# Down projections with their two plain products first in each round, and the third tile of tokens finished one tile of sums sooner

## The chip, the cores and the metric

The kernel runs on one core of one Trainium2 chip. A core has five engines with a queue each: TensorE (PE) multiplies matrices, VectorE (DVE), ScalarE (ACT) and GpSimd (POOL) work on tiles, and SyncE (SP) issues most transfers between the device's memory and the on-chip buffer. Each queue is worked off in order, and engines wait for each other by semaphores. Sums of matrix products land in eight banks of 128 x 512 fp32, from which DVE and ACT read them. The metric is the device time of one execution in microseconds (us); of several runs the median is given.

## The reference

A decoder of two layers on 1024 tokens plus 16 meta tokens, all in fp32, width 1024. Layer 0 is a state-space mixer, layer 1 an attention; each is followed by a gated feed-forward part, and the result is normalized once more:

```python
def _conv_ffn(u, w_up, conv_w, conv_b, w_down):
    h = _causal_dwconv(u @ w_up, conv_w, conv_b)
    g, val = jnp.split(h, 2, axis=-1)
    return (jax.nn.silu(g) * val) @ w_down
...
        h = h + _conv_ffn(_rmsnorm(h, ffn_norm[layer]), ffn_w_up[layer], ffn_conv_w[layer],
                          ffn_conv_b[layer], ffn_w_down[layer])
    return _rmsnorm(h, final_norm)[:, N_META:]
```

The hidden width of the feed-forward part is 2816, that is 22 blocks of 128 rows. The change concerns the last product, `... @ w_down` (the down projection, run once for each layer), and the last line (the final norm) of the second layer.

## The kernel before, in words

**Precision.** Every fp32 matrix is split into a high and a low part (`wh`, `wl` for weights, `gh`, `gl` for tokens). A product of fp32 matrices is then three matmuls: high by high, high by low, low by high (`mm3`, lines 171 to 173). The high part is a copy on ACT; the low part is a subtraction of two tiles, on DVE for tokens (`gl`, L1057) and on POOL for weights (`wl`, L1055).

**A down projection** (`down`) works in two parts. The first 16 of the 22 blocks of rows are cut in two halves, and so are the tokens and the 1024 output columns; the product of these 2 x 2 blocks is made with seven block products instead of eight (Winograd's form of Strassen's scheme), numbered 1 to 7. The remaining six blocks of rows are multiplied plainly afterwards ("tiles of sums": four tiles of tokens, each with eight output blocks, `accumulate`, L403).

**The seven products.** Their operands are (tokens, weights): product 1 is (b11, a11) and product 2 is (b21, a12), the blocks as they were loaded. The others take sums and differences, which DVE makes in place, one after the other in a chain that starts with product 7: `a21 = a11 - a21` (L1039) and `b12 = b22 - b12` (L1040) for 7; `a21 = a22 - a21` (L1042) and `b11 = b11 + b12` (L1043) for 6; L1045 and L1046 for 5; L1048 for 3; L1050 for 4. The order before is 1, 7, 6, 5, 3, 4, 2.

**Rounds and sets.** The 16 blocks of rows are done in two rounds of two sets each (`Set`). In each round every product is done for set 0 and then for set 1; I call one product of one set a half product. `make` prepares the operands of one half product (the differences, `wh` and `wl`, `gh` and `gl`) while PE works on the half product before. There are three buffers each for `wh` and `wl`, so that the operands of a half product can be made only when the one three steps back is through PE. PE sums both sets of a product in the same bank, and at the second set the bank is taken over into the accumulator `acc` of that product: by a copy on ACT (L1102) where it is the first for 1, 5, 6 and 7, by an addition on DVE otherwise (L1104). The accumulators of products 2, 3 and 4 lie in `h`, which holds the residual stream and is loaded ahead of the second product (L1146).

**Banks.** In the first layer a half product has 8 groups of sums (two tiles of 260 tokens by four output blocks, 48 matmuls of 260 columns), which takes all eight banks. In the second layer it has 4 groups (24 matmuls of 512 columns), which takes four, and the products alternate between two lots of four banks.

**Loading.** `FIRST` is the order in which a set's eight blocks are loaded (g for tokens, w for weights); `NEXT` says behind which product which blocks of the next round are loaded, namely when their buffers have come free. All these transfers are in SP's queue, in order (L1025, L1030).

**After the products** the accumulators are added up (`sums`, L1074), and the four tiles of sums follow. After each tile `after` is called: in layer 1 it is `finish`, which for tiles 0, 1 and 2 calls `finish_tokens`: squares on ACT (L239), their sums on POOL and DVE, sums over the rows on PE (L1479), the factor 1/rms (`token_rstd`: L222, a logarithm and an exponential on ACT, L223 and L224, then L225 to L228), transposes on PE (L1487), scaling by the factor and by the gain (L1489, L1490, L1492), and a transfer to the output (L1493). Each tile of 256 tokens is two chunks of 128. The fourth tile is finished by `finish_last`, woven in with its own sums (L1508 to L1542).

**What sets the order.** The attention's order is written out by hand. Elsewhere a scheduler, which simulates the engines with its own durations, orders the instructions on each queue when the kernel is built. So the change also shows in the order of instructions on each queue, which I read from the built kernels.

Of the kernel before, what the change touches and what calls it, by code (L numbers as in the profile page):

```python
# [13 lines left out]
P = 128  # L14
# [37 lines left out]
FFN = Tokens(0, 0), Tokens(META, HB)  # L52
# [34 lines left out]
class Trunk:  # L87
# [905 lines left out]
    def down(self, layer, gd, hd, pool, after, each=None):  # L993
# [68 lines left out]
        def part(ps, op, f, t, first):  # L1062
            gh, gl, wh, wl = op
            for q in range(2):
                s0, n = wide[t]
                c, e = slice(q * H + f * P, q * H + f * P + P), slice(s0, s0 + n)
                self.mm3(ps[:, :n], wh[:, c], wl[:, c], gh[:, q, e], gl[:, q, e], first and q == 0, not first and q == 1)
# [6 lines left out]
                        behind(tt(acc[x, f], acc[x, f], acc[y, f], op=ADD), self.last_add, "behind the products")  # L1074
                        yield

        FIRST = ("g", 0, 0), ("w", 0, 0), ("g", 1, 1), ("g", 0, 1), ("w", 1, 0), ("w", 1, 1), ("w", 0, 1), ("g", 1, 0)

        NEXT = {5: FIRST[:2], 3: FIRST[2:3] + FIRST[4:5], 4: FIRST[3:4] + FIRST[5:6], 2: FIRST[6:]}
        rounds = [[Set(s) for s in (r, r + 1)] for r in range(0, NW // 2, 2)]  # L1080

        def load(sets, what):
            for kind, i, j in what:
                for x in sets:
                    (x.load_g if kind == "g" else x.load_w)(i, j)

        load(rounds[0], FIRST)
        h = [self.Q("h") for _ in range(KD)]
# [9 lines left out]
        def add(i, f, t, ps, first):  # L1098
            s0, n = wide[t]
            x = acc[i, f][:, s0 : s0 + n]  # L1100
            if first and i in (1, 5, 6, 7):
                nc.scalar.activation(x, ps[:, :n], AF.Copy)  # L1102
            else:
                self.last_add = tt(x, x, ps[:, :n], op=ADD)  # L1104
# [4 lines left out]
        def weights(b, hi, lo):  # L1109
            w32 = self.wp.tile([P, 1024], F32, tag="w32", name=self.nm("w32"))  # L1110
            nc.sync.dma_start(w32, a["w_down"][layer, b])
            nc.scalar.activation(hi, w32, AF.Copy)
            pt(lo, w32, hi.bitcast(F32), op=SUB)  # L1113
            ws.append((hi, lo))

        def tokens(x):

            us[x] = []
            for b in rows:
                t = self.Q("g", F32R)  # L1120
                hi, lo = t[:, :S], t[:, QW // 2 : QW // 2 + S]
                nc.sync.dma_start(lo.bitcast(F32), gd[b, :, S * x : S * x + S])
                nc.scalar.activation(hi, lo.bitcast(F32), AF.Copy)
                tt(lo, lo.bitcast(F32), hi.bitcast(F32), op=SUB)
                us[x].append((hi, lo))

        own = lambda: (pool.tile([P, 1024], F32R, tag=z, name=self.nm(z)) for z in ("fh", "fl"))
        common = lambda: (self.wp.tile([P, 1024], F32R, tag=z, name=self.nm(z)) for z in ("wh", "wl"))
        plan = [(r, i, x) for r in range(len(rounds)) for i in (1, 7, 6, 5, 3, 4, 2) for x in range(2)]
        made = {}  # L1130

        def make(n):
            if n < len(plan):
                r, i, x = plan[n]
                made[n] = rounds[r][x].operands(i)
                if r + 1 < len(rounds) and i in NEXT:
                    load([rounds[r + 1][x]], NEXT[i])

        make(0)
        for m in range(0, len(plan), 2):  # L1140
            r, i, _ = plan[m]
            last = r + 1 == len(rounds)
            ps = {}
            if r == 0 and i == 7:
                for f in range(KD):
                    nc.sync.dma_start(h[f][:, : 2 * S] if f < 4 else h[f][:, half(0)], hd[f] if f < 4 else hd[f, :, half(0)])  # L1146
            if last and i == 2:
                h22 = [self.Q("h22") for _ in range(2)]
                h22 = [h22[f // 2][:, f % 2 * S : f % 2 * S + S] for f in range(4)]
                for f in range(4):  # L1150
                    nc.sync.dma_start(h22[f], hd[4 + f, :, half(1)])
            for x in range(2):
                make(m + x + 1)
                if last and i == 4 and x:
                    weights(rows[0], *own())
                if last and i == 2 and not x:
                    tokens(0)
                    weights(rows[1], *own())
                    weights(rows[2], *(self.Q(z, F32R)[:, :D] for z in ("wh", "wl")))
                    for b in rows[3:]:  # L1160
                        weights(b, *common())
                for n, (t, f) in enumerate((t, f) for t in range(len(wide)) for f in range(4)):
                    if x == 0:
                        ps[t, f] = kinds[(m // 2 * 4 * len(wide) + n) % 8]("acc")
                    part(ps[t, f], made[m + x], f, t, x == 0)
                    if x == 1:
                        add(i, f, t, ps.pop((t, f)), r == 0)
                del made[m + x]
# [294 lines left out]
    def finish(self, h, j):  # L1463
        if j == 0:
            self.gfin = self.wp.tile([P, D], F32, tag="w32", name="gfin")
            self.nc.sync.dma_start(self.gfin, self.a["final_norm"].to_broadcast([P, D]))
        if j < 3:
            self.finish_tokens(h, [(t, P) for t in range(FFN[1].tile * j, FFN[1].tile * (j + 1), P)])

    def finish_tokens(self, h, chunks):  # L1470

# [160 lines left out]
```

## Time and profile before

| | us |
|---|---|
| median of 3 runs | 3002.04 |
| lowest and highest of them | 2996.2, 3002.11 |
| the profiled execution | 2999.73 |
| span of the profile | 2998.0 |
| first down projection, products | 1362 to 1538 |
| second down projection, products | 2732 to 2901 |
| its tiles of sums and the end | 2901 to 2998 |

The profile is one execution with start and duration of every instruction. A view by windows counts the instructions of a stretch and gives the TensorE clock that was granted (1.00 is full speed); the view of waits sums, for an instruction that stood idle, which instruction released it; the timeline lists instructions in order, with the idle time before them and its releaser in brackets; the chain of waits is the path that ended last. The profiled execution took 1.73 us more than its span, and 2.31 us less than the median.

### The profile page before, as it was taken

What the parts mean: (1) busy time and instruction counts of PE and PEld (TensorE: products, weight loads), DVE (VectorE), ACT (ScalarE), POOL (GpSimd) and SP (SyncE); (2) the same over time, 40 slices, a digit from 0 to 9 for tenths busy, and PEclk for the clock granted to TensorE, in tenths of its full rate; (3) what the DMA queues carried; (4) which work ended last, traced back from release to release, by engine and by line L of the source; (5) the groups of instructions that cost most, each with busy time, mean ns of one, the idle gap of its engine ahead of it and who ended that gap; (6) DMA issues with size and microseconds to landing.
All of it is one profiled execution on the core that took longest, in us unless ns stands there. A gap on an engine that the chain in (4) does not pass through costs nothing. (4 is left out here: it accounts for less than half of the span.)

```text
span 2998.0 us, 57316 instructions
## 1 busy us (share of the span) xinstructions
PE 2881.1 (96%) x21863; PEld 2737.4 (91%) x21863; DVE 2303.7 (77%) x4026; ACT 1646.3 (55%) x3403; POOL 1309.6 (44%) x1250
## 2 busy tenths in 40 slices
PE   7999999989998999999999999999899999998998
PEld 4999898979998999999999999999798999997878
DVE  5586868886369887878876888888739888888775
ACT  4555555553145556555334888888736555555433
POOL 1254444542334666663443222222343676673441
PEclk9999999999999999999999999999999999999999
DMA  5233333323222222235232122222332222225331
GB/s 162 69 107 90 105 95 100 108 69 135 70 75 70 79 75 82 79 99 180 64 126 84 55 65 62 65 69 55 123 122 65 78 80 84 78 75 173 105 104 59
DMA packets 123411, 272.72 MB, mean 91 GB/s; under 512 B 13664, under 2 KB 53216, under 8 KB 123136
## 3 DMA queue, kind: packets, MB, share of 16 engines
q1 hardware_dynamic: 117760, 257.93, 27.4%
q10 hardware_dynamic: 4112, 6.56, 0.7%
q8 instruction: 172, 2.82, 0.4%
q0 software_dynamic: 1264, 4.57, 0.4%
q14 instruction: 103, 0.84, 0.1%
HBM read 200.89 MB, written 53.20 MB: 85 GB/s over the span
## 5 line engine op out<-in xcount | busy, mean ns | idle before, releaser
L171 PE MATMUL pj<-uh,wh 128*128 128x348 f32 (+2 forms) x1536 | 505.5, 329 | 12.0 <-ACT bk L629 6.1
L172 PE MATMUL pj<-ul,wh 128*128 128x348 f32 (+2 forms) x1536 | 498.6, 325 | 0.0
L173 PE MATMUL pj<-uh,wl 128*128 128x348 f32 (+2 forms) x1536 | 495.9, 323 | 0.0
L171 PE MATMUL p<-bh,fh 128*128 128x262 f32 (+1 forms) x1408 | 401.4, 285 | 6.8 <-DVE c L296 2.8
L173 PE MATMUL p<-bh,fl 128*128 128x262 f32 (+1 forms) x1408 | 401.6, 286 | 3.4 <-POOL fl L905 3.4
L172 PE MATMUL p<-bl,fh 128*128 128x262 f32 (+1 forms) x1408 | 402.4, 286 | 0.1
L905 POOL TENSOR_TENSOR fl<-x,fh 128x1024 fp32r<-128x1024 f32 x88 | 212.5, 2416 | 259.8 <-ACT fh L904 207.6
L172 PE MATMUL p<-bl,wh 128*128 128x262 f32 (+1 forms) x1056 | 301.2, 285 | 6.2 <-DVE bl L857 6.1
L171 PEld LDWEIGHTS pj<-uh,wh 128*128 128x128 f32 x1536 | 292.1, 190 | 15.6 <-ACT xbc L293 4.6
L171 PE MATMUL p<-bh,wh 128*128 128x262 f32 (+1 forms) x1056 | 302.4, 287 | 0.9 <-ACT bh L856 0.9
L173 PE MATMUL p<-bh,wl 128*128 128x262 f32 (+1 forms) x1056 | 301.3, 285 | 0.0
L165 POOL TENSOR_TENSOR wl<-w,wh 128x1024 fp32r<-128x1024 f32 (+2 forms) x76 | 155.2, 2044 | 317.9 <-ACT wh L164 317.8
L172 PEld LDWEIGHTS pj<-ul,wh 128*128 128x128 f32 x1536 | 292.2, 190 | 1.7 <-issue 0.8
L173 PEld LDWEIGHTS pj<-uh,wl 128*128 128x128 f32 x1536 | 291.8, 190 | 1.0 <-issue 0.8
L296 DVE SCALAR_TENSOR_TENSOR c<-p,params,c 128x260 f32<-128x260 f32 (+1 forms) x528 | 250.4, 481 | 47.3 <-ACT c L293 36.9
L171 PEld LDWEIGHTS p<-bh,fh 128*128 128x128 f32 x1408 | 268.7, 191 | 7.9 <-ACT c L293 4.9
L173 PEld LDWEIGHTS p<-bh,fl 128*128 128x128 f32 x1408 | 268.7, 191 | 4.1 <-POOL fl L905 4.0
L172 PEld LDWEIGHTS p<-bl,fh 128*128 128x128 f32 x1408 | 268.1, 190 | 1.1 <-DVE bl L857 0.7
L947 DVE TENSOR_TENSOR c<-c,c 128x260 f32<-128x260 f32 (+1 forms) x176 | 242.0, 1377 | 5.0 <-ACT c L943 2.0
L952 ACT ACTIVATE ft<-p 128x262 f32<-128x262 f32 (+1 forms) x352 | 126.3, 382 | 204.3 <-DVE p L955 181.4
L1055 POOL TENSOR_TENSOR wl<-w,wh 128x1024 fp32r<-128x1024 f32 x56 | 147.5, 2637 | 207.9 <-ACT wh L1054 205.7
L172 PE MATMUL acc<-gl,wh 128*128 128x260 f32 (+1 forms) x672 | 217.9, 325 | 14.7 <-DVE gl L1057 14.7
(325 smaller groups left out, 8473.0 us busy)
## 6 DMA issues: line engine op xcount, KB each, us to landing
w<-in_w_up SPq DMA_DIRECT2D x88, 512.0 KB
w<-in_w_down SPq DMA_DIRECT2D x44, 512.0 KB
w<-in_w_in SPq DMA_DIRECT2D x40, 512.0 KB
E<-ea_d SPq DMA_DIRECT2D x32, 464.0 KB
D<-acs_d SPq DMA_DIRECT2D x32, 420.5 KB
g<-c SPq DMA_DIRECT2D x88, 130.0 KB
g<-c SPq DMA_DIRECT2D x88, 128.0 KB
b<-g SPq DMA_DIRECT2D x16, 520.0 KB
```

Source lines behind the costliest of these rows:

```text
L165: nc.gpsimd.tensor_tensor(wl[:, :n], w32[:, :n], wh[:, :n].bitcast(F32), op=ALU.subtract)
L171: mm(out, wh, uh, start=first, stop=False, skip_group_check=joins)
L172: mm(out, wh, ul, start=False, stop=False, skip_group_check=joins)
L173: mm(out, wl, uh, start=False, stop=last, skip_group_check=joins)
L296: nc.vector.scalar_tensor_tensor(out, ps[:, o + i : o + i + n], wcol(i), out, op0=ALU.mult, op1=ALU.add)
L905: tt(lo[:, :n], t, hi[:, :n].bitcast(F32), op=ALU.subtract)
L947: self.last_up = tt(g[:, :FN], g[:, :FN], v[:, :FN], op=ALU.mult)
L952: nc.scalar.activation(s[:, :N], ps[:, :N], AF.Copy)
L1055: pt(wl, y, wh.bitcast(F32), op=SUB)
```

## The change

It has two parts. The order of the products becomes 1, 2, 7, 6, 5, 3, 4; the loads follow: b21 and a12 come right after b11 and a11, and in the next round b21, a12 and a21 are loaded behind product 3, b22, b12 and a22 behind product 4. What was tied to the place of a product (loading `h` ahead of the second one, the last weights and tokens at the last one) keeps its place in the order. And `finish` is called with other tiles: after the second tile of sums it finishes tiles 0 and 1, after the third tile 2, after the fourth nothing. The computation is the same.

```diff
-        FIRST = ("g", 0, 0), ("w", 0, 0), ("g", 1, 1), ("g", 0, 1), ("w", 1, 0), ("w", 1, 1), ("w", 0, 1), ("g", 1, 0)
-
-        NEXT = {5: FIRST[:2], 3: FIRST[2:3] + FIRST[4:5], 4: FIRST[3:4] + FIRST[5:6], 2: FIRST[6:]}
+        PRODUCTS = 1, 2, 7, 6, 5, 3, 4
+        FIRST = ("g", 0, 0), ("w", 0, 0), ("g", 1, 0), ("w", 0, 1), ("g", 1, 1), ("g", 0, 1), ("w", 1, 0), ("w", 1, 1)
+
+        NEXT = {5: FIRST[:2], 3: FIRST[2:4] + FIRST[6:7], 4: FIRST[4:6] + FIRST[7:]}
...
-        plan = [(r, i, x) for r in range(len(rounds)) for i in (1, 7, 6, 5, 3, 4, 2) for x in range(2)]
+        plan = [(r, i, x) for r in range(len(rounds)) for i in PRODUCTS for x in range(2)]
...
-            if r == 0 and i == 7:
+            if r == 0 and i == 2:
...
-            if last and i == 2:
+            if last and i == 4:
...
-                if last and i == 4 and x:
+                if last and i == 3 and x:
...
-                if last and i == 2 and not x:
+                if last and i == 4 and not x:
...
-        if j < 3:
-            self.finish_tokens(h, [(t, P) for t in range(FFN[1].tile * j, FFN[1].tile * (j + 1), P)])
+        for i in {0: (0, 1), 1: (2,)}.get(j, ()):
+            self.finish_tokens(h, [(t, P) for t in range(FFN[1].tile * i, FFN[1].tile * (i + 1), P)])
```

Beside the three places that it touches, the two down projections and the end, the order of instructions on every queue is as before.

## The prediction

> **What bounds the kernel now.** The page's head says that TensorE is busy nearly all the time.
>
> ```profile
> span 2998.0 us, 57316 instructions
> PE 2881.1 (96%) x21863; PEld 2737.4 (91%) x21863; DVE 2303.7 (77%) x4026; ACT 1646.3 (55%) x3403; POOL 1309.6 (44%) x1250
> ```
>
> So only what lets PE stand, or slows it, can be won. I next read the view by windows for PE's matmuls into `acc`, cut at the down projections. Columns: the window, its length, busy time with the number of matmuls, then the granted clock.
>
> ```profile
> 1362.00:1408.00 46.00, 38.81 (x305) 0.96 0.36 124
> 1408.00:1460.00 52.00, 52.00 (x436) 1.00 0.43 134
> 1460.00:1500.00 40.00, 36.15 (x287) 0.96 0.04 14
> 2732.00:2793.00 61.00, 53.10 (x210) 0.92 0.40 135
> 2793.00:2870.00 77.00, 77.00 (x334) 1.00 0.19 62
> ```
>
> An undisturbed stretch of the first down projection does 436/52 = 8.38 matmuls per us, of the second 334/77 = 4.34. At these rates the 305 at its head need 36.4 us and took 46: **9.6 us lost**. The 210 need 48.4 and took 61: **12.6 us lost**. The 287 in round two need 34.2: 5.8 us lost. What PE waited for, first in the window 1300 to 1600, then in 2700 to 2998 (columns: total us, times, longest):
>
> ```profile
> PE acc L172 <- DVE gl L1057: 6.8, 3, 4.2
> PE acc L171 <- DVE p L1104: 3.9, 2, 2.2
> ```
>
> ```profile
> PE acc L172 <- DVE gl L1057: 7.9, 2, 4.9
> ```
>
> At the heads PE stands 6.8 and 7.9 us for the low part of a token operand; the rest of the losses (2.8 and 4.7) is the slow clock behind the waits, about 1 us a wait in the first and 2.3 in the second. In round two it stands 3.9 us for a bank that DVE has not yet added up. Both times DVE is late. Why it is late at the second head, from the timelines of DVE, POOL and ACT:
>
> ```profile
> 2733.68 2.75 DVE L947 TENSOR_TENSOR c<-c,c 128x256 f32<-128x256 f32 x2 [1.39 <-ACT c L943]
> 2737.72 1.22 DVE L1039 TENSOR_TENSOR w<-w,w 128x1024 f32<-128x1024 f32 x1
> 2738.86 1.22 DVE L1040 TENSOR_TENSOR b<-b,b 128x1024 f32<-128x1024 f32 x1
> ...
> 2741.13 3.44 DVE L1040 TENSOR_TENSOR b<-b,b 128x1024 f32<-128x1024 f32 x1
> 2744.49 3.36 DVE L1043 TENSOR_TENSOR b<-b,b 128x1024 f32<-128x1024 f32 x1
> 2747.77 1.21 DVE L1057 TENSOR_TENSOR gl<-b,gh 128x1024 fp32r<-128x1024 f32 x1
> ```
>
> ```profile
> 2733.42 2.40 POOL L1055 TENSOR_TENSOR wl<-w,wh 128x1024 fp32r<-128x1024 f32 x1 [18.10 <-ACT wh L1054]
> 2740.16 6.60 POOL L1055 TENSOR_TENSOR wl<-w,wh 128x1024 fp32r<-128x1024 f32 x2 [4.34 <-ACT wh L1054]
> 2806.82 2.40 POOL L1055 TENSOR_TENSOR wl<-w,wh 128x1024 fp32r<-128x1024 f32 x1 [2.81 <-ACT wh L1054]
> 2812.39 2.41 POOL L1055 TENSOR_TENSOR wl<-w,wh 128x1024 fp32r<-128x1024 f32 x1 [3.17 <-ACT wh L1054]
> ```
>
> ```profile
> 2732.28 1.06 ACT L1054 ACTIVATE wh<-w 128x1024 fp32r<-128x1024 f32 x1 [1.03 <-DMA w<-in_w_down]
> 2739.02 1.06 ACT L1054 ACTIVATE wh<-w 128x1024 fp32r<-128x1024 f32 x1 [4.92 <-issue]
> ```
>
> A DVE operation on two tiles follows the next at 1.14 us (2737.72 to 2738.86), but each of POOL's two `wl` makes one of them take 3.4: **they run by turns**, and each `wl` that falls among them costs DVE 2.25 us. So between 2737.72 and 2747.77 DVE did 5 operations (5.7) and paid for two `wl` (4.5). A half product is 2812.39 - 2806.82 = 5.57 us of PE here. In the first layer:
>
> ```profile
> 1367.48 1.22 DVE L1039 TENSOR_TENSOR w<-w,w 128x1024 f32<-128x1024 f32 x1
> 1429.76 2.09 DVE L1104 TENSOR_TENSOR h<-h,acc 128x260 f32<-128x260 f32 x6
> ...
> 1363.16 2.40 POOL L1055 TENSOR_TENSOR wl<-w,wh 128x1024 fp32r<-128x1024 f32 x1 [17.57 <-ACT wh L1054]
> 1430.29 2.40 POOL L1055 TENSOR_TENSOR wl<-w,wh 128x1024 fp32r<-128x1024 f32 x1 [3.38 <-ACT wh L1054]
> 1436.02 2.41 POOL L1055 TENSOR_TENSOR wl<-w,wh 128x1024 fp32r<-128x1024 f32 x1 [3.33 <-ACT wh L1054]
> ```
>
> A half product is 5.73 us (1436.02 - 1430.29), and six additions out of a bank take 0.35 each although a `wl` runs beside them: those do not take turns.
>
> **Part 1, second down projection.** No instruction is added or removed; product 2 moves ahead of 7. DVE gains two half products before PE asks for a difference, but in the built order of DVE's queue the low part for product 2, set 1 now stands eighth behind the end of the up projection: two L1039, two L1040, two L1043, one L1042, then it. (For set 0 it stands among the last operations of the up projection, with time to spare.) PE asks for it after three half products and eight matmuls that do without (as many stand ahead of it in PE's queue): 2732 + 3 x 5.57 + 8/4.34 = 2750.5. When is it there? POOL's second `wl` had to wait in the profile until ACT could begin at 2739.02, since product 1 held a buffer. Product 2's set 0 has a free buffer and weights that came early, so its `wl` now follows at once at 2735.8 and takes turns with the up projection's last L947, as 2733.68 shows (2.75 for two of 0.4). I let DVE start 2.1 us later, at 2739.8 (bounds: 0 and 4.5, one more `wl` in it). Eight operations: 2739.8 + 9.1 = 2748.9. Among them fall the `wl` of product 2 set 1 (from 2740.1), of product 7 set 0 (buffer free after two half products, 2743.1, plus ACT: 2744.3) and of 7 set 1 (2749.9): 3 x 2.25 = 6.8. So 2755.7, a wait of 5.2, with 2.3 for the clock: 7.5 of the 12.6 stay. Behind it, product 7's low parts are two and three operations later, in time, and product 6's after it, with 1 or 2 us to spare; its sums have banks of their own. **Gain 5.1**; bounds: 12.6 if DVE is in time (2739.8 less 2.1, one `wl` among the eight: 2749.0), 0 if two more `wl` come before it.
>
> **Part 1, first down projection.** The same, but the low part in question stands seventh, and PE asks for it at 1362.4 + 3 x 5.73 + 4/8.38 = 1380.1. DVE started at 1367.48; the moved `wl`, at 1365.6 behind the one at 1363.16, puts that off to about 1370.2. Then 7 x 1.14 = 8.0 and two `wl`: 1382.7, a wait of 2.6. PE is through with product 2 at 1388. Now the banks: product 7 needs the ones of product 2, all eight are in use, and they come free by DVE's L1105 (L1104 before) instead of ACT's copies, which did it for product 1. In DVE's built queue the first of these additions stands behind five more operations (two L1057, L1042, L1046, L1045): 1382.7 + 5.7 + 2.25 to 4.5 = 1390.7 to 1392.9. That is **a new wait** of 2.7 to 4.9, say 4. The other additions stand in two lots behind one to two operations, and PE has three groups of both sets to do meanwhile. With the clock, about 1 us for the small wait and 2.3 for the larger, 2.6 + 4 + 3.3 = 9.9 against 9.6 lost before: **gain 0**, bounds -5 (every one of the five takes 3.4) and 9.6 (no wait).
>
> **Part 1, the rest.** In round two the differences of 6, 5 and 3 lie among the additions of 2 and 7 instead of 1 and 7, in the same pattern: its 5.8 us stay, +-3. `h` is asked for at product 2 now, not 3; its transfers are issued after the last L947, 2 to 3 us later, ten us before the additions. The loads of the next round come behind products 3 and 4, two products ahead of 7, as before. I cost them at 0; if a load were late it would hold DVE's queue and then a bank.
>
> At one place the Trainium skill is weighed. "TensorE: Matmul & The Clock Gate", section "What's actually happening", says that the clock halves after an idle window of about 3.4 us. By that rule the 2.6 us wait would cost no clock, and the sum would be 1 us lower.
>
> ```profile
> 1480.00:1490.00 10.00, 7.80 (x53) 7.59 (x52) 8.53 (x10) 2.98 (x3) 3.81 (x2) 0.83 0.16 52
> ```
>
> That window holds only the wait of 2.2 (the longest on L1104 above), and its clock is 0.83: 1.7 us beside the idle time. I keep the row.
>
> **Part 2, the end.** The last sums are in `h` at 2980.92.
>
> ```profile
> 2980.92 0.42 DVE L403 TENSOR_TENSOR h<-h,acc 128x256 f32<-128x256 f32 x1 [0.57 <-PE acc L173]
> 2982.71 0.16 DVE L222 TENSOR_SCALAR fs<-fs 128x2 f32<-128x2 f32 x1 [1.37 <-PE fs L1535]
> 2988.14 0.48 DVE L1540 SCALAR_TENSOR_TENSOR y<-fin,ty,gfin 128x256 f32<-128x256 f32 x1
> ...
> 2960.62 0.16 DVE L222 TENSOR_SCALAR fs<-fs 128x2 f32<-128x2 f32 x1 [0.36 <-PE fs L1479]
> 2962.14 0.75 DVE L1492 SCALAR_TENSOR_TENSOR y<-fin,ty,gfin 128x512 f32<-128x512 f32 x1
> ```
>
> ```profile
> 2981.69 2.54 ACT L239 ACTIVATE sq<-h 128x256 f32<-128x256 f32 x8
> 2985.55 0.20 ACT L223 ACTIVATE ty<-fs 128x2 f32<-128x2 f32 x1
> ```
>
> ```profile
> 2988.95 0.99 SPq L1542 DMA_DIRECT2D out<-y  x2
> 2992.16 2.22 SPq L1493 DMA_DIRECT2D out<-y  x2
> ```
>
> ```profile
> 2959.79 0.79 PE fs L1479 x8
> 2963.18 0.44 PE fin L1487 x4
> ```
>
> Tile 3's row sums were ready at 2982.71, but ACT first made tile 2's eight squares (L239) and loaded a table, until 2985.55; tile 3 was scaled from 2988.14. Unhindered, the way from L222 to scaling takes 2962.14 - 2960.62 = 1.5, so 2984.2: 3.9 earlier. The two transfers of L1542 then come at 2985.05 and 2985.55, and nothing follows. In the profile the last transfer began about 0.4 before 2994.38 and the span ended at 2998.0, 4 us on; mine ends at 2989.6, or up to 1.5 later as it shares with its twin: 2990.3, 7.7 us earlier. For that PE does tile 2's eight row sums and 16 transposes amid its work: 0.79 + 4 x 0.44 = 2.6. **Gain 5.1**; bounds 3.5 and 6.5 (the twin, the shares of PE). Tile 1, one tile of sums earlier too, adds no work; DVE, ACT and POOL have room there.
>
> **Sum**: 5.1 + 0 + 5.1 = 10.2; 2999.7 becomes 2989.5, and against the median, 2.3 above the profiled run, 2991.8: I say **2992**.
>
> **Rivals.** (a) *DVE is in time.* The moved `wl` falls where DVE idles, or DVE's turn comes first: both heads lose nothing, 3002 - 9.6 - 12.6 - 5 = 2975. For: the chain needs 8.0 and 9.1 us and has 12.6 and 12.8 from its old start. Against: 3.44 and 3.36 above. The Trainium skill, "SBUF — State Buffer", section "Who interferes with whom", speaks against it: whichever of the two engines issues first holds the shared ports for its whole instruction; the turns above agree. (b) *The wait only moves.* As many `wl` come before the low part as were in front of product 7: heads 0, the end alone, 2997. For: DVE and POOL do the same work, in turns. (c) *The banks decide: slower.* In the first layer each of the five operations ahead of the first addition, and of the three ahead of the next two lots, meets a `wl` (8 x 2.25 instead of 2 x 2.25, 13.5 us more); if (b) holds too, 3002 + 13.5 - 5 = 3010. It decides from about 5 more meetings on. Against: one `wl` per half product.
>
> **How the numbers follow.** Forecast 0.55 (2986 to 2997 by itself), (a) 0.17, (b) 0.20, (c) 0.08. A run of this kernel tells some 0.2% (6 us) from no change: faster is below 2996.0. It gets 0.49 of the forecast, all of (a) and 0.06 of (b): 0.72. Slower, (c) less a little: 0.07. Same: 0.21. Range: to most of (b) above, 3000, and two thirds of the way to (a) below, 2979.
>
> **What would show it.** After: at the heads PE waits for L1057 once at each, about 2.6 and 5 us (zero: (a)); in the first, for L1105 at product 7, about 4 us (over 10: (c)); the L1042 or L1043 ahead of it at 3.4; the last transfer issued by L1543, with L223 0.3 us after L222. Wrong would be a wait for a transfer in round two, or for banks by the transposes of tiles 1 and 2.

## The result, and the profile after

The changed kernel takes **2993.85 us** (median of 20 runs, 2985.09 to 3000.25), the kernel before 3001.98 (20 runs): the ratio is **0.9974, 95% interval 0.9966 to 0.9983**, or 7.8 us less (5.1 to 10.2). The forecast was 2992, 10.2 us less. A second measurement beside other kernels (below) gave 0.9975 (0.9966 to 0.9983).

The head of the page after the change: the span, and the busy time of the engines.

```profile
span 2994.1 us, 57318 instructions
PE 2879.0 (96%) x21863; PEld 2738.0 (91%) x21863; DVE 2304.0 (77%) x4026; ACT 1653.4 (55%) x3403; POOL 1308.0 (44%) x1250
```

The span is 3.9 us shorter, half of what the medians say. One execution can't show 8 us in its span: over the fourteen profiled executions of the table below, the time up to the first down projection went from 1359 to 1367 us and the stretch between the two from 1190 to 1197, whatever the kernel. So I compare the stretches that the change touches, from the first matmul of a down projection to its last product. The timeline of PE in the changed kernel gives them:

```profile
1363.43 0.28 PE L171 MATMUL acc<-gh,wh 128*128 128x260 f32 x1
...
1539.60 0.29 PE L173 MATMUL acc<-gh,wl 128*128 128x260 f32 x1
...
2734.52 0.39 PE L171 MATMUL acc<-gh,wh 128*128 128x512 f32 x1
...
2900.57 0.40 PE L173 MATMUL acc<-gh,wl 128*128 128x512 f32 x1
```

So the first down projection takes 1539.89 - 1363.43 = 176.5 us and the second 2900.97 - 2734.52 = 166.5; from there to the end of the span are 93.1. The same three stretches in every profiled kernel (us; the kernels are told of below):

| kernel | first down | second down | to the end | ratio to before (95% interval) |
|---|---|---|---|---|
| before | 176.1 | 169.1 | 97.0 | 1 |
| changed | 176.5 | 166.5 | 93.1 | 0.9974 (0.9966 to 0.9983) |
| changed, again (e8) | 178.4 | 165.8 | 94.5 | 0.9975 (0.9966 to 0.9983) |
| e1, order in first layer alone | 176.7 | 169.3 | 96.4 | 0.9996 (0.9984 to 1.0007) |
| e2, order in second layer alone | 175.1 | 164.6 | 97.1 | 0.9979 (0.9969 to 0.9989) |
| e3, end alone | 176.5 | 168.8 | 93.9 | 0.9974 (0.9965 to 0.9984) |
| e11, end alone, again | 175.5 | 168.6 | 92.5 | 0.9981 (0.9972 to 0.9989) |
| e4, 8 wl by DVE | 170.1 | 162.5 | 91.7 | 0.9925 (0.9909 to 0.9940) |
| e5, product 2's operands early | 176.4 | 164.7 | 94.2 | 0.9982 (0.9974 to 0.9991) |
| e6, product 2's sums by ACT | 171.6 | 166.8 | 95.0 | 0.9959 (0.9947 to 0.9972) |
| e7, tail order on ACT | 184.1 | 163.6 | 90.1 | 0.9965 (0.9952 to 0.9979) |
| e9, three edits together | 167.1 | 157.1 | 90.1 | 0.9907 (0.9891 to 0.9923) |
| e10, all 56 wl by DVE | 161.2 | 156.8 | 87.1 | **0.9871 (0.9858 to 0.9884)** |
| e12, old order, all wl by DVE | 161.7 | 157.2 | 87.3 | 0.9876 (0.9859 to 0.9892) |

A stretch that a kernel leaves as it was repeats within 1.4 us: 175.1 to 176.5, 168.6 to 169.3, 96.4 to 97.1. Against their means (175.8, 168.9, 96.85) the two traces of the changed kernel have +0.7 and +2.6 in the first, -2.5 and -3.2 in the second, -3.7 and -2.3 at the end: 5.5 and 2.9 us less in all, where the interval of the medians begins at 5.1. The ratios rest on 20 executions of the changed kernel, 11 or 12 each of e1, e2, e3, e5, e8 and e11, and only 4 to 6 of the others.

What PE waits for in the changed kernel, from its timeline (the bracket has the wait and who ended it):

```profile
1370.81 0.35 PE L171 MATMUL acc<-gh,wh 128*128 128x260 f32 x1 [1.36 <-DVE c L296]
1383.64 0.39 PE L172 MATMUL acc<-gl,wh 128*128 128x260 f32 x1 [0.74 <-DVE gl L1057]
1394.15 0.56 PE L171 MATMUL acc<-gh,wh 128*128 128x260 f32 x1 [4.95 <-DVE h L1105]
...
2758.39 0.80 PE L172 MATMUL acc<-gl,wh 128*128 128x512 f32 x1 [5.13 <-DVE gl L1057]
2890.00 0.50 PE L173 MATMUL acc<-gh,wl 128*128 128x512 f32 x1 [1.74 <-POOL wl L1055]
```

In the first layer the waits for product 7's low part are gone and one of 4.95 for a bank stands in their place. In the second, two waits of 4.9 and 3.0 became one of 5.13 at product 2 and a new one of 1.74 near the end. DVE and POOL at that second head:

```profile
2742.55 1.22 DVE L1039 TENSOR_TENSOR w<-w,w 128x1024 f32<-128x1024 f32 x1
2743.69 3.43 DVE L1040 TENSOR_TENSOR b<-b,b 128x1024 f32<-128x1024 f32 x1
2747.05 3.44 DVE L1039 TENSOR_TENSOR w<-w,w 128x1024 f32<-128x1024 f32 x1
2750.41 1.21 DVE L1040 TENSOR_TENSOR b<-b,b 128x1024 f32<-128x1024 f32 x1
2751.54 4.52 DVE L1043 TENSOR_TENSOR b<-b,b 128x1024 f32<-128x1024 f32 x2
2755.99 1.21 DVE L1042 TENSOR_TENSOR w<-w,w 128x1024 f32<-128x1024 f32 x1
2757.12 1.21 DVE L1057 TENSOR_TENSOR gl<-b,gh 128x1024 fp32r<-128x1024 f32 x1
```

```profile
2736.55 4.95 POOL L1055 TENSOR_TENSOR wl<-w,wh 128x1024 fp32r<-128x1024 f32 x2 [18.65 <-ACT wh L1054]
2742.65 3.39 POOL L1055 TENSOR_TENSOR wl<-w,wh 128x1024 fp32r<-128x1024 f32 x1 [1.16 <-ACT wh L1054]
2746.82 2.58 POOL L1055 TENSOR_TENSOR wl<-w,wh 128x1024 fp32r<-128x1024 f32 x1 [0.78 <-ACT wh L1054]
2752.40 2.58 POOL L1055 TENSOR_TENSOR wl<-w,wh 128x1024 fp32r<-128x1024 f32 x1 [3.00 <-ACT wh L1054]
```

Eight operations of DVE take 15.8 us, of which 9.1 are their own: two of 3.4 and one of two that together take 4.5 lie beside the three `wl`. That is the forecast's sum, term by term.

### The profile page after: what moved, and what is told of

It reads as the page before. It is cut to its first block, busy times and chain, and to the rows that moved or that the text cites. A ratio compares the mean times of both kernels' runs of the same rounds, so it can differ in the third digit from the quotient of the medians.

```text
span 2994.1 us, 57318 instructions
## 1 busy us (share of the span) xinstructions
PE 2879.0 (96%) x21863; PEld 2738.0 (91%) x21863; DVE 2304.0 (77%) x4026; ACT 1653.4 (55%) x3403; POOL 1308.0 (44%) x1250
## 3 DMA queue, kind: packets, MB, share of 16 engines
q10 hardware_dynamic: 4112, 6.56, 0.7%
## 4 chain that ended last, share of the span: by engine, by line
PE 77%; DVE 12%; issue 4%; ACT 3%; POOL 2%; DMA 2%; SPq 0%; DVEq 0%; ACTq 0%; POOLq 0%
PE p L172 9%; PE p L171 9%; PE p L173 9%; PE acc L172 6%; PE acc L171 6%; PE acc L173 6%; PE pj L171 6%; PE pj L172 6%; PE pj L173 6%; PE po L1366 3%; PE lg L1325 3%; PE wT L1352 2%; DVE D L598 1%; PE ms L831 1%; DVE xbc L545 1%
## 5 line engine op out<-in xcount | busy, mean ns | idle before, releaser
L171 PE MATMUL acc<-gh,wh 128*128 128x260 f32 (+1 forms) x672 | 215.0, 323 | 10.9 <-DVE h L1105 7.2
```

Source lines behind the costliest of these rows:

```text
L171: mm(out, wh, uh, start=first, stop=False, skip_group_check=joins)
```

## The experiments

**The theory**: each `wl` of POOL costs the DVE operation beside it 2.25 us, so DVE is late at the heads, and the new order shifts what waits for it; the end is a gain of its own. **Rivals**: the order of DVE's queue decides, not POOL; the long DVE operations come from the transfers that arrive then; the end alone carries the gain.

**The parts alone (e1, e2, e3, e11).** The order and what goes with it (the order of loads, the places of `h` and of the remaining rows) are made to depend on the layer, or the end is left as before.

```
e1: fresh = layer == 0     e2: fresh = layer == 1     e3, e11: fresh = False
    PRODUCTS = (1, 2, 7, 6, 5, 3, 4) if fresh else (1, 7, 6, 5, 3, 4, 2)
...
e1, e2: finish_tokens as before, a tile behind each of j = 0, 1, 2     e3, e11: as changed
```

> The new order of products in the first layer alone; second layer and end as before. The forecast's ledger (gain 0 there, bounds -5 to 9.6): 3002, ratio 1.000; the stretch from the first matmul of that down projection to its last product takes 176, as in both traces (175.9 and 176.2), with one wait of some 5 us for the additions of product 2 (L1105) in place of those for L1057. Rival (c), banks decide: slower, 1.002 to 1.003. Rival (a), the heads lose nothing: 0.997.

Measured: 0.9996, the stretch 176.7, the same waits as in the changed kernel (1.77, 0.74, 4.95). The forecast's 0 stands.

> The new order in the second layer alone; first layer and end as before. The forecast's ledger (gain 5.1, bounds 0 to 12.6): ratio 0.998, the stretch of that down projection 163.6; by the trace of the changed kernel it is 166.1 (2.6 less than the 168.7 of before), ratio 0.999, with one wait of 5 us for L1057 at product 2 and one of 1.7 for the low part of a weight block (L1055) near the end. Rival (b), the wait only moves: 168.7, ratio 1.000.

Measured: 0.9979, the stretch 164.6, which is 4.3 under the mean of the old order; one wait of 4.2 at product 2, one of 1.75 near the end. The forecast's 5.1 stands within a microsecond, with some luck: the wait of 1.75 is not in it, and the clock from 2750 to 2770, behind the other wait, is 0.91 in this trace, 1.8 us, where the changed kernel has 0.83, 3.4 us.

> The new end alone; both down projections as before. The forecast's ledger (gain 5.1, bounds 3.5 to 6.5): ratio 0.9983; from the last product of the second down projection to the end of the span 92.3; by the trace of the changed kernel 93.5 (97.4 before), ratio 0.9987. Rival (b) says that this is the whole of the change's gain: ratio 0.9974, as measured for the change.

Measured: 0.9974, the stretch 93.9. Time and trace disagreed, so it was run again.

> The end alone once more. Its time said 7.8 us less (0.9974), its trace 3.0 to 3.7 in the stretch that it changes (93.9 against 96.4 to 97.1). If the trace's stretch is the effect, the ratio is 0.9988 to 0.999 and the stretch 93 to 94; if the time is, 0.9974 again, and something outside that stretch is faster by 4 us.

Measured: 0.9981, the stretch 92.5. Two traces give 3.0 and 4.4 us, two timings 7.8 and 5.7.

Rival (b), by which the end alone carries the gain, falls: the second layer's order alone is worth 4.3 us by trace and 6.3 by time, about as much as the end alone (3.7 and 6.7, each the mean of two). **By time the parts add up to more than the whole**: 1.2, 6.3 and 6.7 make 14 us, with an interval of about 5 either way, against 7.5 to 7.8 for all of them together. That is barely beyond the noise, and e1, e2 and e3 are compared with one and the same set of runs of the kernel before, whose median (3003.6) is the highest of the sets measured, so an error in it counts in each. By the traces they make 7 (0.9 lost, 4.3 and 3.7 won). What the rest is stays open.

**POOL's wl (e4).** One line: who makes the low part of a weight block.

```
-                pt(wl, y, wh.bitcast(F32), op=SUB)
+                (tt if i in (2, 7) and me.k < 4 else pt)(wl, y, wh.bitcast(F32), op=SUB)
```

> The changed kernel, with the low parts wl of products 2 and 7 of round one made by DVE and not by POOL (four operations a layer). If DVE's operations on two tiles and POOL's run by turns, each wl costs DVE 1.14 instead of 2.25, no operation at the heads takes 3.4 beside them, and the low part gl of product 2, set 1, stands tenth and is ready at about 2752 instead of 2758: the wait of 5.1 is under 1, the stretch of the second down projection 159 to 161 instead of 166, the time 5 us under the changed kernel's (some of it may be lost again to a longer wait near the end). If DVE's 3.4 have another cause (the transfers that come in at the same time), they stay, four operations are added, and the wait grows by 2 to 4 us: 170, the time above the changed kernel's.

Measured: **0.9925**, 15 us under the changed kernel, where 5 were expected, with four operations more on DVE at each head. By the stretches 12 us are won: 6.4 in the first layer, 4.0 in the second and 1.4 behind it. The second stretch, 162.5, is 1.5 over what was expected; waits of 0.84 and 1.77 near its end are in it. Its DVE, at the second head, in the timeline:

```profile
2740.50 1.22 DVE L1040 TENSOR_TENSOR b<-b,b 128x1024 f32<-128x1024 f32 x1
2741.64 1.22 DVE L1043 TENSOR_TENSOR b<-b,b 128x1024 f32<-128x1024 f32 x1
2742.77 1.22 DVE L1055 TENSOR_TENSOR wl<-w,wh 128x1024 fp32r<-128x1024 f32 x1
2743.91 1.22 DVE L1043 TENSOR_TENSOR b<-b,b 128x1024 f32<-128x1024 f32 x1
2745.04 1.22 DVE L1055 TENSOR_TENSOR wl<-w,wh 128x1024 fp32r<-128x1024 f32 x1
2746.30 1.23 DVE L1042 TENSOR_TENSOR w<-w,w 128x1024 f32<-128x1024 f32 x1
2747.44 1.22 DVE L1057 TENSOR_TENSOR gl<-b,gh 128x1024 fp32r<-128x1024 f32 x1
```

Nothing takes 3.4: the same operations, with the same transfers in the program, run 1.14 apart. (One `wl` on DVE that falls beside the one `wl` left to POOL there takes 2.58.) The long operations were POOL's doing, and the rival of the transfers falls. The low part is ready 18.3 us after the first matmul (2748.66 - 2730.39), and PE has no wait at product 2. That also brings back most of rival (a): once DVE is in time, the second head keeps one wait of 0.97, at product 6, and the first one of 1.25 for a bank.

**The place in DVE's queue (e5).** Product 2's operands for set 1 are issued ahead of the copies of product 1's sums.

```
-                make(m + x + 1)
+                if m + x != 2:
+                    make(m + x + 1)
...
+                if m + x == 1:
+                    make(3)
+                for g in groups:
+                    add(*g)
```

> The changed kernel, with the four operations that make product 2's operands for set 1 written ahead of the copies of product 1's sums instead of behind them; in the built order its low part gl then lies inside the up projection, and not eighth behind it. If the place in DVE's queue decides (the forecast's step), PE does not wait at product 2; gl of product 7, set 0, is eighth now, ready at the old time, 24 us after the first matmul of the down projection, and PE asks for it at 24.1: the wait of 4 to 5 us and its clock go, the stretch of the second down projection is 159 to 161 (less a longer wait near the end), of the first 175 (its wait for the banks stays at 4 to 5); time 5 to 7 under the changed kernel's. If DVE's work as such decides and the wait only moves (rival b), it stands at product 7 with 4 to 5 us and nothing is gained.

Measured: 0.9982, no better than the changed kernel; a miss. PE in its second layer, and at the first layer's bank:

```profile
1394.95 0.56 PE L171 MATMUL acc<-gh,wh 128*128 128x260 f32 x1 [6.56 <-DVE h L1105]
...
2756.31 0.50 PE L172 MATMUL acc<-gl,wh 128*128 128x512 f32 x1 [0.56 <-DVE gl L1057]
2777.24 0.50 PE L172 MATMUL acc<-gl,wh 128*128 128x512 f32 x1 [3.43 <-DVE gl L1057]
2884.20 0.50 PE L171 MATMUL acc<-gh,wh 128*128 128x512 f32 x1 [1.53 <-ACT wh L1054]
2886.70 0.50 PE L173 MATMUL acc<-gh,wl 128*128 128x512 f32 x1 [1.76 <-POOL wl L1055]
```

The wait at product 2 is gone; in its place stand 0.56 at product 7, the next one, and 3.43 at product 6, 21 us later; the waits near the end grew from 1.7 to 3.3; in the first layer the bank wait grew from 4.95 to 6.56. Rival (b) was right for this edit: with the same work on DVE, a wait taken away at one product appears at another.

**The banks (e6).**

```
-            if first and i in (1, 5, 6, 7):
+            if first and (i in (1, 5, 6, 7) or i == 2 and layer == 0):
...
+                    if layer == 0:
+                        for f in range(4):
+                            tt(acc[2, f], acc[2, f], h11[f], op=ADD)
```

> The changed kernel; in the first layer the sums of product 2 in round one are copied out of their banks by ACT, and the residual of those 4 x 260 columns is added by DVE at the end of the projection. If the wait of 4.95 at product 7 is for banks that DVE frees late, it falls under 1 and its clock with it: the first down projection takes 168 to 170 instead of 176.5, the rest is as in the changed kernel, ratio to it 0.9975. If PE would be held by the differences of product 7 anyway, a wait for L1057 of 3 to 5 stands in its place, and the stretch stays over 174.

Measured: 0.9959, the stretch 171.6, and no wait for L1105 or L1057 at this head: the 4.95 were for banks that DVE had not yet read. The stretch is 1.6 over what was expected, and a wait of 2.5 for a bank of the up projection (1.4 in the changed kernel) is in it; the ratio to the changed kernel beside it is 0.9984, not 0.9975.

**The tail (e7).** ACT and POOL ahead of the wait of 1.74 in the changed kernel:

```profile
2872.77 1.04 ACT L1054 ACTIVATE wh<-w 128x1024 fp32r<-128x1024 f32 x1
2884.26 1.30 ACT L1124 ACTIVATE g<-g 128x512 fp32r<-128x512 f32 x2 [10.44 <-DMA g<-g]
2885.46 1.05 ACT L1113 ACTIVATE fh<-w 128x1024 fp32r<-128x1024 f32 x1
2886.41 1.04 ACT L1054 ACTIVATE wh<-w 128x1024 fp32r<-128x1024 f32 x1
```

```profile
2887.58 5.17 POOL L1055 TENSOR_TENSOR wl<-w,wh 128x1024 fp32r<-128x1024 f32 x2 [7.41 <-PE acc L172]
```

ACT stands 10.4 us at a transfer of token rows, and the copy of a weight for product 4 is queued behind it. POOL's row names PE as what it waited for, though it began 0.13 after ACT's copy ended at 2887.45. The edit, at the two kinds of ACT's copies for the remaining rows:

```
-            nc.scalar.activation(hi, w32, AF.Copy)
+            behind(nc.scalar.activation(hi, w32, AF.Copy), self.last_wh, "behind the products")
...
-                nc.scalar.activation(hi, lo.bitcast(F32), AF.Copy)
+                behind(nc.scalar.activation(hi, lo.bitcast(F32), AF.Copy), self.last_wh, "behind the products")
```

> The changed kernel, with ACT's copies of the remaining token rows and weights (L1113, L1124) behind its last copy of a weight for the products. If the wait of 1.7 for L1055 near the end of the second down projection comes from ACT, which stands at a token transfer with that copy behind it, the wait goes and the stretch is 1.5 to 2 shorter (163 to 165); if it is POOL's or the buffer's, it stays. What follows the products can lose up to 1 us, since the copies held back come later. No difference in the time that can be told.

Measured: 0.9965. In the second layer the wait went (163.6), and what follows was not later but 3 us sooner (90.1). In the first layer the stretch grew to 184.1: PE waits twice there for banks, behind DVE's low parts of token rows.

```profile
1531.12 0.58 PE L171 MATMUL acc<-gh,wh 128*128 128x260 f32 x1 [2.47 <-DVE h L1105]
1533.90 0.59 PE L171 MATMUL acc<-gh,wh 128*128 128x260 f32 x1 [1.10 <-DVE h L1105]
```

```profile
1525.11 5.62 DVE L1125 TENSOR_TENSOR g<-g 128x520 fp32r<-128x520 f32 x2
1530.65 0.41 DVE L1105 TENSOR_TENSOR h<-h,acc 128x260 f32<-128x260 f32 x1
```

**The change again (e8).**

> The changed kernel once more, beside the others on one chip. The three parts alone gave 0.9996, 0.9979 and 0.9974, some 15 us together, the change as a whole 7.8. If the parts add up, this run gives 0.995; if they do not, 0.997 to 0.998 again. The stretches should be as in its first trace: 176.5, 166.5 and 93.1, and by them 6 to 7 us below before.

Measured: 0.9975, stretches 178.4, 165.8, 94.5: the first result holds; the sum of the parts, 0.995, does not come. In this execution one more wait, of 1.5, for L1105 near the end of the first projection.

**Together, and all of them (e9, e10).** e9 has e4, e6, and e7 for the second layer alone. e10 is the changed kernel with one line: `tt(wl, y, wh.bitcast(F32), op=SUB)`, all low parts of the products' weights by DVE.

> The changed kernel with three of the edits that helped: the low parts wl of products 2 and 7 of round one by DVE (both layers), the sums of product 2 in round one copied by ACT in the first layer (the residual added later), and ACT's copies of the remaining rows behind the last weight for the products in the second layer alone. If the losses are separate, as the traces say: first down projection 168 to 170 (170.1 with the first edit alone, which left a wait of 1.3 for the banks), second 160 to 161 (162.5 less the waits of 0.8 and 1.8 near its end), the end 90 to 91; 5 us under the run with the first edit alone, ratio to before 0.990 to 0.991. If they share one cover, nothing is added: 0.9925.

Measured: 0.9907, stretches 167.1, 157.1, 90.1. By the stretches the losses are separate: each is shorter than in e4, by 3.0, 5.4 and 1.6 us. The first two are also shorter than expected, by 1 and 3 us. The time alone can't tell: its interval overlaps e4's.

> The changed kernel with all 56 low parts wl of the products by DVE, not eight. If every wl of POOL holds a DVE operation for 2.25 and costs 1.14 as DVE's own, the waits for L1105 in round two (1.6 and 2.3 in every run so far) shrink too, and both down projections are 2 to 4 us shorter than with the eight moved (170.1 and 162.5). If away from the heads POOL's wl mostly fall into DVE's idle time, the 48 others add 1.14 each to DVE: those waits grow by 1 to 3 us each, and the stretches are longer than 170.1 and 162.5.

Measured: **0.9871, 2963.4 us**, the shortest of all: 30 us under the changed kernel with a one-line edit. The two stretches are 8.9 and 5.7 below e4's, where 2 to 4 were expected at best, and the end is 4.6 below: there PE's wait of 2.3 for an addition of DVE (L403) in the tiles of sums has shrunk to 0.5. The waits for L1105 in round two, which had stood in every kernel until then, are gone; one wait of over 0.4 us (0.43) is left in both projections. The head of its page:

```profile
span 2959.1 us, 57265 instructions
PE 2864.9 (97%) x21863; PEld 2726.5 (92%) x21863; DVE 2295.0 (78%) x4082; ACT 1647.3 (56%) x3403; POOL 1161.1 (39%) x1194
```

DVE has 56 operations more, 56 x 1.14 = 64 us of work, and is busy 9 us **less** than in the changed kernel (2295.0 against 2304.0): the other operations take 73 us less, 1.3 for every `wl` moved. So the cost was not at the heads alone. Not all of the 30 us need come straight from DVE's turns: near the end of the second projection ACT now stands at most 1.7 us at a transfer of token rows (10.4 in the changed kernel), and its built order differs in places. What that is worth was not measured by itself.

**The old order without POOL's wl (e12).**

> The kernel before with the new end, and with all 56 low parts wl of the products by DVE: against the run before it only the order of the products differs. If what DVE did at the heads was lost to POOL's wl, then without them even product 7 as the second is nearly in time: its low part stands seventh in the built order (three operations of L1039 and L1040 more than one wl and one L1043 ahead), ready 5.1 + 7 x 1.14 = 13.1 after the first matmul of the first down projection against 11.9, and 5.8 + 8.0 = 13.8 against 13.0 in the second: a wait of about 1 in each. The stretches are 162 to 164 and 158 to 160, and the order of the products is worth 1 to 3 us a layer. If the order carries the gain, waits of 4 or more stay at product 7 and again behind it, and the stretches are 167 and 163 or longer.

Measured: 0.9876 against 0.9871 for e10, stretches 161.7 and 157.2 against 161.2 and 156.8, one wait of 0.5. With POOL out of the way the order of the products is worth 0.5 us a layer, which is less than the 1 to 3 expected and within the scatter of a stretch: it had treated a symptom.

## Why the prediction was right, and which terms were off

The time came within 2 us of the forecast (2993.85 against 2992), but not by its terms: as the traces show them they add up to 5.5 and 2.9 us, where the forecast has 10.2. So a part of the agreement is luck.

- **Second down projection, gain 5.1**: 2.5 and 3.2 in the two traces, 4.3 alone. The mechanism came out as worked out: DVE starts 8.0 us after PE (7.8 forecast), eight operations take 15.8 (15.9), PE waits 5.13 and 4.8 (5.2). Two terms failed. The clock behind this wait is 0.83 from 2750 to 2770 in the changed kernel, 3.4 us, where I had 2.3. And "the rest at 0" has the wait of 1.74 for `wl` near the end, which was no step of mine. In the profile before, ACT stands at the same transfer, and the copy at the same place of the order begins as late:

```profile
2886.08 1.04 ACT L1054 ACTIVATE wh<-w 128x1024 fp32r<-128x1024 f32 x1
```

  But its `wl` ended at 2889.60 and PE asked for it at 2890.15. In the changed kernel PE asked 1.9 earlier, at 2888.26, and `wl` ended at 2889.95: a PE that comes earlier meets ACT's queue standing at a transfer. e7 showed that it is ACT's queue.
- **First down projection, gain 0**: 0.7 and 2.6 lost, 0.9 alone. The bank wait I put at 4 was 4.95, and the wait of 2.6 for the low part came as 0.74 plus 1.36 for a bank of the up projection. The moved `wl` already held DVE's last operations there, two of 0.4 that took 4.95 beside two `wl`, in the timelines of DVE and POOL:

```profile
1364.57 4.95 DVE L947 TENSOR_TENSOR c<-c,c 128x260 f32<-128x260 f32 x2 [0.51 <-ACT c L943]
```

```profile
1364.31 4.93 POOL L1055 TENSOR_TENSOR wl<-w,wh 128x1024 fp32r<-128x1024 f32 x2 [17.72 <-ACT wh L1054]
```

  In e4 that wait is gone; e6 showed the banks.
- **Round two, the same**: its waits are 1.62 and 2.31 in place of 1.65 and 2.20. One of 0.65, at product 4 of round one, is new.
- **End, gain 5.1**: 2.3 to 4.4 by four traces. The way from the last sums in PE to the end of the span is 17.1 before and 9.4 after, 7.7 less (7.7 forecast). What falls short is PE's time ahead of that: from the last product to the last sum PE takes 79.2 to 81.0 in the kernels with the old end, 83.2 to 85.1 in the traces of the change and of the end alone, 4 us more where 2.6 were forecast. PE's added work is not the reason. Eight of the 16 transposes and the eight row sums take from 2953.82 to 2955.45, 1.63, and all of them some 2.4:

```profile
2953.82 0.60 PE L1488 MATMUL fin<-ident,h 128*128 128x128 f32 x4
2954.25 0.95 PE L1480 MATMUL fs<-one,sq 128*128 128x1 f32 x8
2955.07 0.63 PE L1488 MATMUL fin<-ident,h 128*128 128x128 f32 x4
2955.45 0.36 PE L172 MATMUL acc<-g,wh 128*128 128x256 f32 x1
```

  The rest is the clock, which the forecast left out at this place. Both kernels wait the same 2.29 us for L403 some 15 us after the last product; the view by windows has, before and after,

```profile
2915.00:2925.00 10.00, 8.50 (x72) 1.00 0.17 52
2915.00:2925.00 10.00, 8.79 (x61) 0.83 0.17 52
```

  A clock of 0.83 over 10 us is 1.7 us, and 2.4 + 1.7 is the 4 us. The new end is not shown to be the cause of the slow clock: of the three kernels with the old end e2 has it too (0.83 from 2910 to 2920) and takes 81.0, and e10 and e12, which have the new end and a short wait here, keep 1.00. Why the clock fell in one trace and not in the other stays open.

The rivals: (a), DVE in time, came true only when POOL's `wl` went (e4, e10); (b), the wait only moves, was right for e5; (c), banks decide, named the right place, but its price did not come: 4.95 in all, where it wanted 13.5 more.

The 3.4 that became 1.14 in e4 bears out the turns. The Trainium skill, "SBUF — State Buffer", section "Who interferes with whom", has one of the two engines hold the shared ports for its whole instruction; the trace agrees.

What a wait costs in clock did not follow from its length here. Two kernels wait the same 2.3 us in round two, and show

```profile
1490.00:1500.00 10.00, 7.69 (x65) 1.00 0.16 54
```

in the changed kernel (clock 1.00, and 1.00 from 1500 to 1510 too; wait of 2.31 from 1496.24), and in e4

```profile
1490.00:1500.00 10.00, 7.72 (x52) 0.83 0.16 52
```

(clock 0.83, wait of 2.28 from 1492.40). The Trainium skill, "TensorE: Matmul & The Clock Gate", section "What's actually happening", puts the slow clock behind about 3.4 us of idling. By that rule neither wait should cost clock; the one in e4 did. For the first layer the forecast kept 1 us of clock for its wait of 2.6 and 2.3 for the bank. In the changed kernel

```profile
1364.00:1390.00 26.00, 23.10 (x189) 1.00 0.44 161
1390.00:1400.00 10.00, 5.85 (x32) 0.66 0.01 2
```

the waits of 1.36 and 0.74, which lie ahead of 1390, cost no clock, and the 4.95 cost 3.4 us. The sum of the two, 3.3, was right by luck.

## What to carry to other kernels

When two engines run by turns, an operation on the second one is not free for the first: price it as what it takes from the engine that is short (2.25 here where the two meet, 1.3 on average over all 56) against doing it there (1.14), before reordering anything. A new order of the same work moved waits here, to the next product (e5) or to the end of the projection; look for what makes the late engine late. Compare the stretches that an edit touches, not spans, where one execution scatters by as much as the edit is worth.

## What the runs showed that was not expected

- Moving 56 operations onto the busier engine (DVE, 77%) from one at 44% shortened the kernel by 30 us and lowered DVE's own busy time by 9.
- The waits of 1.6 and 2.3 in round two, the same within some 0.1 in every kernel before e10, came from POOL as well: they are gone in e10 and e12.
- A copy that is held back on ACT (e7) cost 6 to 8 us in the first layer and gained about 6 in the second, with the same edit.
